# Forget sums broadcast by DMA and masked on GpSimd, in place of two TensorE products for each pair of heads

## The chip, the cores and the metric

The kernel runs on one core of a Trainium2 chip. A core has five engines with instruction streams of their own: TensorE (PE in the profile; PEld is its weight load), VectorE (DVE), ScalarE (ACT), GpSimd (POOL) and SyncE (SP), which here only issues DMAs. Each engine takes its instructions in order, and semaphores order the engines among themselves. The metric is device time in microseconds (us) of one execution; lower is better.

## The reference, cut to what matters

Two layers over 256 tokens of width 1024. Each layer has eight heads of sparse attention (called NSA), eight heads of forgetting attention (called fox) and an MLP with squared ReLU. The change touches the fox heads:

```
log_f = log_sigmoid(f_logits + f_bias)
cum = cumsum(log_f, axis=1)                      # one row of 256 sums for each head
logits = q @ k.T * scale + cum[:, q, None] - cum[:, None, k]
p = softmax(where(k <= q, logits, -1e30))
```

The term cum[q] is the same for a whole row, so it drops out of the softmax. What is left to add is, for each head, one row of -cum[k] that is the same for all 128 queries of a tile, and the causal mask. The kernel works with scores times 8 and undoes it by a factor of -0.125.

## The kernel before, in words

The tokens form two tiles of 128 rows. All weights are split into two parts (whi, wlo) that TensorE multiplies in three products in a reduced float32 form; scores and transposes are full float32 products, which take several passes. A weight unit arrives as a DMA on SP's queue into one of nine buffers with the tag "raw" (RBUFS, line 48). ScalarE copies it into whi, VectorE subtracts to get wlo (`Weights.get`, lines 485 to 508), and the raw buffer is free again.

In each layer: six chunks of the input projection (c0 to c5), the sparse and the forgetting attention interleaved with the later chunks, the output projection (eight units w_out 0 to 7; the first four are worked in between the attention steps, the last four behind them), and the MLP. The attention runs over a list `flat` (line 1322) of 16 NSA tiles and 8 fox tiles. Step i issues the scores of tile i, scales tile i-1, transposes tile i-2, and multiplies with the values from tile i-3; `fill` puts pieces of the stream of chunks and w_out units between them. For a tile, VectorE does the mask-add (`tensor_tensor_reduce` in `scores`, lines 1197 to 1200: score plus mask, times -0.125, with the row minimum), ScalarE the exps, VectorE the scaling, TensorE the three transposes. `side` (line 1324) puts further work behind certain steps; the forget sums stand behind step 8.

The forget sums before (`forget_sums`, line 1023): two products give the running sums in PSUM, with each head's row repeated every 32 rows; ScalarE copies them into hi (reduced form) and rest, and VectorE makes of these the tile cum, in which alternating blocks of 32 rows hold the high and the low part. In `fox_scores` (line 1157) a pair of heads gets its scores by eight float32 passes on 64-row tiles, and then, for each head, one 64x384 product of selr (a column that picks the head's rows, high and low) with cum adds the row of sums to all 128 rows in PSUM.

The order of the instructions is not that of the code. A Recorder keeps every operation; all are issued at line 404, so that line stands in every row of the profile, and groups are told apart by tiles. `schedule` (line 297) is a list scheduler over modelled durations (`_cost`, line 446; for a DMA the bytes over 360 per ns, line 453, plus LATE). It takes buffers of one tag in the order in which the code first used them (`fits`, line 326), so a later raw buffer is never handed out ahead of an earlier one. `order` (line 282) keeps the best of five passes. The result is fixed when the kernel is built.

Of the kernel before, what the change touches and what calls it, by code (L numbers as in the profile page):

```python
# [18 lines left out]
F32 = mybir.dt.float32  # L19
F32R = mybir.dt.float32r  # L20
AF = mybir.ActivationFunctionType
# [114 lines left out]
class View:  # L136
# [21 lines left out]
    def bitcast(self, dtype):  # L158
        return self._with(lambda ap: ap.bitcast(dtype), dtype=dtype)

    def mask(self):
        m = np.zeros(self.buf.size, bool)
        m[self.ix.ravel()] = True
        return m
# [13 lines left out]
class Recorder:  # L178
    def __init__(self, nc, tc):
        self.nc, self.tc = nc, tc  # L180
        self.ops, self.fifo, self.key, self.hot, self.lane, self.group = [], {}, None, False, None, None
        self.after = None
        for e in ("tensor", "vector", "scalar", "sync"):
            setattr(self, e, _Engine(self, e))

    def tile(self, pool, shape, dtype, name, tag=None, bufs=1, psum=False):
# [110 lines left out]
    def schedule(self):  # L297
# [5 lines left out]
        for op in self.ops:  # L303
            op.missing, op.ready, op.start = len(op.deps), 0.0, None
            for b in op.bufs:
                left[b] = b.ops
        waiting = {e: [] for e in ("tensor", "vector", "scalar", "sync")}
        busy = dict.fromkeys(waiting, 0.0)
        bus, tiled = 0.0, (P, P)
        for op in self.ops:  # L310
# [135 lines left out]
def _cost(op, views):  # L446

    out = op.args[0] if op.args else op.kw["out"]
    n = int(np.prod(out.shape[1:]))
    part = 100 * (out.shape[0] < P)  # L450
    if op.engine == "sync":
        v = views[0][1]
        return v.shape[0] * int(np.prod(v.shape[1:])) * 4 / 360.0
    if op.engine == "tensor":
        if op.name == "stretch":
            side = P // min(op.tile)
            return sum(_product(*x[:2], side) for x in op.args[2][::side])
        return _product(op.name, op.args, 1)
    if op.engine == "vector":
        if op.name == "reciprocal":  # L460
            return 60 + 6.5 * n
        if op.name == "tensor_reduce":
            n = int(np.prod(op.args[1].shape[1:]))
        fast = op.name in ("tensor_copy", "tensor_scalar", "memset") and not any(v.buf.psum for _, v in views)
        aps = sum(isinstance(v, View) for v in op.args[2:4]) if op.name == "tensor_scalar" else int(
            op.name == "scalar_tensor_tensor" and isinstance(op.args[2], View))
        return 68 + part + 64 * aps + n * (0.52 if fast else 1.04) + 10 * (op.name == "tensor_tensor_reduce")
    src = op.args[1]
    aps = sum(isinstance(op.kw.get(k), View) for k in ("bias", "scale", "accum_out"))
    return n / 1.2 + (55 if src.buf.psum else 92) + 93 * aps  # L470
# [52 lines left out]
def trunk(nc, A, consts_in, out, sbp, pp):  # L523
    def tile(shape, dtype, name, tag=None, bufs=1):
        return nc.tile(sbp[(tag or name) not in OPERANDS], shape, dtype, name, tag, bufs)
# [251 lines left out]
        if k == 0:  # L777
            nc.vector.tensor_copy(gcol, gcol0)

    selr = tile([P, 8], F32R, name="selr")  # L780
    ident_r = tile([P, P], F32R, name="identr")
    r_mix = [None, None]
    carry = None
# [1 line left out]
    for l in range(DEPTH):  # L785
# [143 lines left out]
        def hidden_gelu(s):  # L929
            u, z = T["gu" + s], T["gz" + s]  # L930
            nc.vector.tensor_scalar(z, z, 1.0, None, op0=OP.add)
            nc.vector.reciprocal(z, z)
            h = small([P, 2, 32], "gh")
            nc.vector.tensor_mul(h, u, z)
            T["gh" + s] = h
# [86 lines left out]

        def forget_sums():


            ps = psum("s")
            f = [x.rearrange("p a b -> p (a b)") for x in lf]
            nc.tensor.matmul(ps[:, :S], f[0], cst[:, C_TRI:C_TRI + S], start=True, stop=False)
            nc.tensor.matmul(ps[:, P:S], f[1], cst[:, C_TRI:C_TRI + P], start=False, stop=True)
            cum = tile([P, 384], F32R, name="cum", tag="cum")  # L1030
            two = tile([P, 2, S], F32R, name="two", tag="rl", bufs=2)
            hi, rest = two[:, 0], two[:, 1].bitcast(F32)
            nc.scalar.activation(hi, ps[:, :S], AF.Copy)
            nc.scalar.activation(rest, ps[:, :S], AF.Copy, scale=cst[:, C_REST:C_REST + 1])
            for o, n in ((0, P), (P, S)):
                nc.vector.scalar_tensor_tensor(cum[:, o:o + n], hi[:, :n].bitcast(F32), cst[:, C_REST + 1:C_REST + 2],
                                               rest[:, :n], op0=OP.mult, op1=OP.add)
            T["cum"] = cum


        def in_chunk(c, evac, by_token=False):
# [114 lines left out]

        def fox_scores(pair):


            ps = [psum("s") for _ in range(2)]  # L1160
            rows = [slice(par * HD, par * HD + HD) for par in range(2)]
            with nc.stretch():
                for o, n, q0 in ((0, 128, 0), (128, 256, 128)):
                    for par, h in enumerate(rows):
                        nc.tensor.matmul(ps[par][:, o:o + n], T["fqT"][h, pair, q0:q0 + P], T["fkT"][h, pair, 0:n],
                                         start=o == 0, stop=False, skip_group_check=True)
                for par, h in enumerate(rows):
                    i = 2 * pair + par
                    nc.tensor.matmul(ps[par][:, 0:384], selr[h, i:i + 1].to_broadcast([HD, P]), T["cum"][h],
                                     start=False, stop=True, skip_group_check=True)  # L1170
            return [(x[:, 0:128], x[:, 128:384]) for x in ps]

        def nsa_scores(e):
# [11 lines left out]
        def scores(e):  # L1185
            kind, pair, par, br = e[:4]
            if kind == "fox":
                if par == 0:
                    T["sc"] = fox_scores(pair)
                ps = T["sc"][par]  # L1190
            else:
                if br == 1:
                    T["sc"] = nsa_scores(e)
                ps = T["sc"][br - 1]
            p = small([P, 384], "pr", 3)
            st = small([P, 4], "st", 4)
            for a, b, t in SEGS:
                nc.vector.tensor_tensor_reduce(
                    out=p[:, a:b], in0=ps[t], in1=cst[:, C_MASK + 256 - (b - a):C_MASK + 256], op0=OP.add, op1=OP.min,
                    scale=-0.125, scalar=3.0e38, accum_out=st[:, t:t + 1])  # L1200
            for a, b, t in SEGS:
                nc.scalar.activation(p[:, a:b], p[:, a:b], AF.Exp, scale=-1.0, bias=st[:, t:t + 1],
                                     accum_out=st[:, 2 + t:3 + t])
            return p, st
# [74 lines left out]
                        r_mix[t] = rsqrt_sum(*squares_of_x(t, "rm"))  # L1279
        row_scales()  # L1280
        if first:
            nc.scalar.activation(selr, cst[:, C_SEL:C_SEL + 8], AF.Copy)
            nc.scalar.activation(ident_r, ident, AF.Copy)

        fill(4)
# [30 lines left out]
        for t in range(NT):  # L1316
# [5 lines left out]
        flat = [("nsa", pair, par, br) for pair in range(4) for par in range(2) for br in (1, 2)]  # L1322
        flat += [("fox", pair, par, 0) for pair in range(4) for par in range(2)]
        side = {0: lambda: fill_to("c3"), 1: compressed_exp, 2: lambda: (compressed_scale(), hidden_T("v")),
                3: lambda: (compressed_T(), hidden_gelu("v")),
                6: compressed_v, 7: compressed_vT, 8: forget_sums, 14: lambda: fill_to("c4"), 17: lambda: fill_to("c5")}
        st = {}
        pTs = {}
        o = None
# [1 line left out]
        for i in range(len(flat) + 4):  # L1331
            if 0 <= i - 1 < len(flat):
                scale(flat[i - 1], *st[i - 1])
            if i < len(flat):
                st[i] = scores(flat[i])
                if i == 15:
                    done.add("nsa")
                    g_post, g_pre2 = load_gains(("g_post_mix", l), ("g_pre_mlp", l))
            fill(1)
            if i in side:  # L1340
                side[i]()
                fill(1)
            if 0 <= i - 2 < len(flat):
                pTs[flat[i - 2]] = probs_T(st.pop(i - 2)[0], i % 2, flat[i - 2])
            fill(1)
            j = i - 3
            if 0 <= j < len(flat) and flat[j][2] == 1 and flat[j][3] != 1:
                kind, pair, par, br = flat[j]
                if pair % 2:
                    o = psum("o")  # L1350
                    if br:
                        nc.tensor.matmul(o, T["vbig"][:, pair // 2], T["pcT"][pair // 2], start=True, stop=False,
                                         skip_group_check=True)
                    cols = lambda q: [(q // 2) * HD] * 2 if br else [2 * q * HD, 2 * q * HD + HD]
                    pv(o, [[([pTs.pop((kind, q, x, b)) for x in range(2)], (fV, vS, vW)[b], cols(q))
                            for b in ((1, 2) if br else (0,))] for q in (pair - 1, pair)], not br)
                    o_evac(o, kind, pair)
            if i >= 12 or i % 2:
                fill(1)
# [203 lines left out]
```

## Time and profile before

| | us |
|---|---|
| median of 3 runs | 622.77 (622.66 to 622.86) |
| the profiled execution, device time | 622.19 |
| its span, first to last instruction | 620.4 |
| VectorE busy | 472.5 |
| ScalarE busy | 382.3 |

The granted clock of TensorE was 0.999 on average. The span leaves out 1.8 us around the first and last instruction. In the profile, out<-in names what an instruction writes and reads; x16 is a count; a timeline row has start, duration, engine, operation, tiles and shape. DMA rows of the page give the median time from issue to landing. A matmul row's duration is from its issue to its modelled end; such products overlap, so their price is the distance between starts.

### The profile page before, as it was taken

The numbers are of one execution on the slowest core, as the hardware profiler recorded it, in microseconds if no ns is written. First come the engines' busy times: TensorE is split into PE (matmuls) and PEld (weight loads), VectorE is DVE, ScalarE is ACT, GpSimd is POOL, SyncE is SP. The second block draws the span as 40 slices with busy tenths as digits, with TensorE's granted clock in tenths as the row PEclk, the third lists the DMA queues.
The fourth block names the chain that finished last, engine by engine and source line by source line (L and its number), as shares of the span: only waits on it lengthen the run. The fifth ranks groups of instructions, "written<-read, shape, count | busy, mean of one in ns | idle before, by whom it ended". The sixth has DMA issues, their size and how long they took to land.

```text
span 620.4 us, 9937 instructions
## 1 busy us (share of the span) xinstructions
PE 612.6 (99%) x3572; PEld 518.6 (84%) x3572; DVE 472.5 (76%) x1043; ACT 382.3 (62%) x730; POOL 0.2 (0%) x4
## 2 busy tenths in 40 slices
PE   9999999999999999999999999999999999999995
PEld 6989987788888888888888998777888888888884
DVE  6889999889976567557598999987996575566544
ACT  7766777577655456555466758765776455556522
POOL 0000000000000000000000000000000000000000
PEclk9999999999999999999999999999999999999999
DMA  8988535218765666664347783532386665655001
GB/s 322 403 312 312 219 105 202 102 37 303 255 189 186 187 204 198 182 197 140 106 139 251 267 328 101 171 104 69 115 296 209 197 196 176 203 190 187 31 1 68
DMA packets 33601, 115.69 MB, mean 186 GB/s; under 512 B 3984, under 2 KB 4112, under 8 KB 33552
## 3 DMA queue, kind: packets, MB, share of 16 engines
q1 hardware_dynamic: 33552, 115.06, 55.5%
q8 instruction: 28, 0.46, 0.3%
q14 instruction: 21, 0.17, 0.1%
HBM read 114.00 MB, written 1.05 MB: 185 GB/s over the span
## 4 chain that ended last, share of the span: by engine, by line
PE 98%; DMA 1%; DVE 0%; ACT 0%; issue 0%; DVEq 0%; SPq 0%
PE s L404 35%; PE acc L404 31%; PE x L404 25%; PE o L404 7%; DMA first<-in_first_dram 1%; DVE x L404 0%; DVE m L404 0%; DVEq L1559 0%; ACT whi L404 0%; DVE rsqrt L404 0%; ACT xT L404 0%; SPq L404 0%; ACT rl L404 0%; DVEq L404 0%
## 5 line engine op out<-in xcount | busy, mean ns | idle before, releaser
L404 DVE TENSOR_TENSOR wlo<-wraw,whi 128x1024 fp32r<-128x1024 f32 (+1 forms) x188 | 225.5, 1201 | 98.7 <-ACT whi L404 58.6
L404 ACT ACTIVATE whi<-wraw 128x1024 fp32r<-128x1024 f32 (+1 forms) x188 | 194.8, 1041 | 106.4 <-PE acc L404 73.5
L404 PE MATMUL s<-xT,whi 128*128 128x512 f32 x448 | 106.5, 390 | 0.0
L404 PEld LDWEIGHTS s<-xT,whi 128*128 128x128 f32 x448 | 83.4, 188 | 16.8
L404 PE MATMUL x<-whi,aT 128*128 128x512 f32 x256 | 88.6, 390 | 0.0
L404 PE MATMUL acc<-whi,aT 128*128 128x512 f32 x256 | 88.3, 389 | 0.0
L404 PEld LDWEIGHTS s<-xT,wlo 128*128 128x128 f32 x448 | 57.4, 191 | 2.2
L404 PE MATMUL s<-xT,wlo 128*128 128x256 f32 x448 | 58.1, 283 | 0.0
L404 PEld LDWEIGHTS acc<-whi,aT 128*128 128x128 f32 x256 | 48.0, 188 | 10.0
L404 PEld LDWEIGHTS x<-whi,aT 128*128 128x128 f32 x256 | 48.1, 188 | 9.6
L404 ACT ACTIVATE pr<-pr,st 128x256 f32<-128x256 f32 (+1 forms) x96 | 42.9, 448 | 19.6 <-DVE st L404 19.3
L404 PE MATMUL x<-wlo,aT 128*128 128x512 f32 x128 | 50.0, 390 | 0.0
L404 PE MATMUL acc<-wlo,aT 128*128 128x512 f32 x128 | 49.9, 390 | 0.0
L404 PE MATMUL acc<-xT,whi 128*128 128x256 f32 x256 | 49.6, 288 | 0.0
L404 PEld LDWEIGHTS acc<-xT,whi 128*128 128x128 f32 x256 | 40.1, 190 | 1.5 <-issue 0.4
L404 PE MATMUL acc<-whi,xT 128*128 128x512 f32 (+1 forms) x128 | 37.5, 353 | 0.0
L404 PE MATMUL acc<-xT,wlo 128*128 128x256 f32 x128 | 36.4, 284 | 0.0
L404 PE MATMUL x<-whi,xT 128*128 128x512 f32 x112 | 36.2, 396 | 0.1
L404 ACT ACTIVATE h<-s 128x256 f32<-128x256 f32 x56 | 21.2, 378 | 16.0 <-PE s L404 16.0
L404 ACT ACTIVATE rl<-h 128x512 f32<-128x512 f32 x28 | 17.7, 633 | 18.0 <-DVE h L404 18.0
L404 PEld LDWEIGHTS acc<-wlo,aT 128*128 128x128 f32 x128 | 24.0, 188 | 5.0
L404 ACT ACTIVATE rl<-x 128x512 f32<-128x512 f32 x24 | 14.7, 612 | 21.8 <-PE x L404 16.7
(221 smaller groups left out, 961.3 us busy)
## 6 DMA issues: line engine op xcount, KB each, us to landing
wraw<-in_w_up_dram SPq DMA_DIRECT2D x64, 512.0 KB, 3.7
wraw<-in_w_down_dram SPq DMA_DIRECT2D x64, 512.0 KB, 3.7
wraw<-in_w_in_dram SPq DMA_DIRECT2D x36, 512.0 KB, 5.1
wraw<-in_w_out_dram SPq DMA_DIRECT2D x16, 512.0 KB, 6.8
w<-in_cmp_w_k_dram SPq DMA_DIRECT2D x8, 512.0 KB, 5.2
w<-in_cmp_w_v_dram SPq DMA_DIRECT2D x8, 512.0 KB, 5.4
first<-in_first_dram SPq DMA_DIRECT2D x7, 384.0 KB, 6.0
wraw<-in_w_in_dram SPq DMA_DIRECT2D x8, 288.0 KB, 4.1
```

Of the source, the lines that this page charges most:

```text
L404: getattr(getattr(self.nc, op.engine), name)(*[real(v) for v in args], **{k: real(v) for k, v in kw.items()})
```

## The change

The two products for each pair are gone, with selr and the split of cum into high and low parts. cum is now a plain float32 tile, copied out of PSUM by two ScalarE copies (128 and 256 columns). The forget sums move from behind step 8 to behind step 4. A new function, called ahead of the scores of every even fox step, takes a raw buffer for a bias tile of 128 x 2 x 384, fills each half by a DMA on SP's queue that reads one row of cum for all 128 rows, and lets GpSimd write -1e30 where the causal mask forbids, in two selects. The mask-add of a fox tile reads this bias where it read the mask. The scheduler learns of GpSimd as a fifth engine.

```
+    def to_rows(self, n):
+        return self._with(lambda ap: ap.unsqueeze(1).to_broadcast([1, n, self.ix.size]))
...
-        waiting = {e: [] for e in ("tensor", "vector", "scalar", "sync")}
+        waiting = {e: [] for e in ("tensor", "vector", "scalar", "gpsimd", "sync")}
...
+    if op.engine == "gpsimd":
+        return 200 + 0.72 * n + 10 * int(np.prod(out.shape[1:-1]))
...
-            cum = tile([P, 384], F32R, name="cum", tag="cum")
-            two = tile([P, 2, S], F32R, name="two", tag="rl", bufs=2)
-            hi, rest = two[:, 0], two[:, 1].bitcast(F32)
-            nc.scalar.activation(hi, ps[:, :S], AF.Copy)
-            nc.scalar.activation(rest, ps[:, :S], AF.Copy, scale=cst[:, C_REST:C_REST + 1])
+            cum = tile([P, 384], F32, name="cum", tag="cum")
             for o, n in ((0, P), (P, S)):
-                nc.vector.scalar_tensor_tensor(cum[:, o:o + n], hi[:, :n].bitcast(F32), cst[:, C_REST + 1:C_REST + 2],
-                                               rest[:, :n], op0=OP.mult, op1=OP.add)
+                nc.scalar.activation(cum[:, o:o + n], ps[:, :n], AF.Copy)
             T["cum"] = cum
+
+        def forget_bias(pair):
+
+            b = tile([P, 2, 384], F32, name="bias", tag="raw", bufs=RBUFS)
+            for par in range(2):
+                i = 2 * pair + par
+                nc.sync.dma_start(b[:, par], T["cum"][i:i + 1, :].to_rows(P))
+            for o in (0, 2 * P):
+                nc.gpsimd.affine_select(out=b[:, :, o:o + P], in_=b[:, :, o:o + P], pattern=[[0, 2], [-1, P]],
+                                        compare_op=OP.is_ge, fill=NEG, base=0, channel_multiplier=1)
+            T["fb", pair] = b
...
-                                         start=o == 0, stop=False, skip_group_check=True)
-                for par, h in enumerate(rows):
-                    i = 2 * pair + par
-                    nc.tensor.matmul(ps[par][:, 0:384], selr[h, i:i + 1].to_broadcast([HD, P]), T["cum"][h],
-                                     start=False, stop=True, skip_group_check=True)
+                                         start=o == 0, stop=o > 0, skip_group_check=True)
...
-                    out=p[:, a:b], in0=ps[t], in1=cst[:, C_MASK + 256 - (b - a):C_MASK + 256], op0=OP.add, op1=OP.min,
+                    out=p[:, a:b], in0=ps[t], in1=T["fb", pair][:, par, a:b] if kind == "fox" else
+                    cst[:, C_MASK + 256 - (b - a):C_MASK + 256], op0=OP.add, op1=OP.min,
...
-                3: lambda: (compressed_T(), hidden_gelu("v")),
+                3: lambda: (compressed_T(), hidden_gelu("v")), 4: forget_sums,
-                6: compressed_v, 7: compressed_vT, 8: forget_sums, 14: lambda: fill_to("c4"), 17: lambda: fill_to("c5")}
+                6: compressed_v, 7: compressed_vT, 14: lambda: fill_to("c4"), 17: lambda: fill_to("c5")}
...
+                if 16 <= i < 24 and i % 2 == 0:
+                    forget_bias(i // 2 - 8)
                 st[i] = scores(flat[i])
```

More of the change, by code (lines that the diff above doesn't have):

```diff
@@ L182, in __init__ @@
         self.after = None
-        for e in ("tensor", "vector", "scalar", "sync"):
+        for e in ("tensor", "vector", "scalar", "gpsimd", "sync"):
             setattr(self, e, _Engine(self, e))
@@ L778, in first_xT @@
             nc.vector.tensor_copy(gcol, gcol0)
-    selr = tile([P, 8], F32R, name="selr")
     ident_r = tile([P, P], F32R, name="identr")
@@ L1281, in trunk @@
         if first:
-            nc.scalar.activation(selr, cst[:, C_SEL:C_SEL + 8], AF.Copy)
             nc.scalar.activation(ident_r, ident, AF.Copy)
```

## The prediction, made before the changed kernel ran

> **What bounds the kernel now.** I read the page from the top: busy shares, slices, chain, and then the view of waits for TensorE alone.
>
> ```profile
> PE 612.6 (99%) x3572; PEld 518.6 (84%) x3572; DVE 472.5 (76%) x1043; ACT 382.3 (62%) x730; POOL 0.2 (0%) x4
> PE   9999999999999999999999999999999999999995
> PEclk9999999999999999999999999999999999999999
> DMA  8988535218765666664347783532386665655001
> PE 98%; DMA 1%; DVE 0%; ACT 0%; issue 0%; DVEq 0%; SPq 0%
> ```
>
> ```profile
> PE o L404 <- DVE warm L404: 1.2, 1, 1.2
> ```
>
> The reader is to see that TensorE is the bound from end to end: 612.6 us of a 620.4 us span, 98% of the chain, full clock, and one wait of 1.2 us in the whole run, for the warm-up tile. So a product taken from TensorE is a gain at its full price, and anything new that TensorE has to wait for is a loss at its full price. DMA is half idle on average, which will turn out to be no cover.
>
> **What goes.** Each of the eight pairs of forgetting heads (four in each layer) loses two 64x384 products.
>
> ```profile
> L404 PE MATMUL s<-cum,selr x16: 518/520/523, 96.3 to 416.7; 64*128 64x384 f32 x16
> ```
>
> ```profile
> 95.73 0.93 PE L404 MATMUL s<-fkT,fqT 64*128 64x128 f32 x8
> 96.30 0.53 PE L404 MATMUL s<-cum,selr 64*128 64x384 f32 x2
> 96.76 0.50 PE L404 MATMUL x<-whi,oT 128*128 128x512 f32 x1
> ...
> 97.34 0.40 PE L404 MATMUL x<-whi,oT 128*128 128x512 f32 x1
> 97.58 0.40 PE L404 MATMUL acc<-whi,oT 128*128 128x512 f32 x1
> 97.81 0.40 PE L404 MATMUL x<-whi,oT 128*128 128x512 f32 x1
> ```
>
> The 520 ns is a latency of pipelined products, not their price. From the start of the pair to the next product are 0.46 us (96.30 to 96.76), but that holds the tail of the score products ahead and the change back to 128x128 tiles, which stay. What leaves is the streaming of 384 columns, for both halves side by side. Products of 512 columns stand 0.235 us apart (97.34, 97.58, 97.81), so 384 columns are 0.18 us. I take 0.18 (upper end 0.46): 8 x 0.18 = **1.4 us off TensorE** (upper end 3.7). Off the bound go four VectorE instructions (415 ns each) and two of four ScalarE copies become narrower; neither engine is waited for, so I cost them at nothing.
>
> ```profile
> L404 DVE SCALAR_TENSOR_TENSOR cum<-two,cst x4: 346/415/485, 82.3 to 387.5; 128x256 fp32r<-128x256 f32 x2, 128x128 fp32r<-128x128 f32 x2
> ```
>
> **What comes.** Per layer: eight DMAs on SP's queue, each writing one 1.5 KB row of cum to all 128 rows (192 KB), and eight selects on GpSimd. The mask-add reads bias in place of the mask: same instruction, same size, nothing. The four bias tiles take four of the nine "raw" buffers that hold arriving weights.
>
> Where they stand decides. In the order of the changed program, SP's queue in each layer has w_out 0, then the first bias DMA, and the remaining seven w_out loads between and behind the others; ahead of w_out 4 stand all eight bias DMAs and w_out 1 to 3. Buffers are handed out in that order, so no later load can overtake. Before, nothing held those loads:
>
> ```profile
> 55.18 6.26 SPq L404 DMA_DIRECT2D wraw<-in_w_out_dram  x8
> ```
>
> All eight w_out loads of layer 0 were issued from 55.2 to 61.4 us. Now the first bias DMA waits for cum, and w_out 1 to 7 are queued behind it on SP. The forget sums move up: in layer 0 they stand right ahead of the third tile's transposes, in layer 1 some five products ahead of them.
>
> ```profile
> 69.25 0.49 PE L404 MATMUL s<-cst,pr 128*128 128x128 f32 x3
> ```
>
> ```profile
> 373.05 0.49 PE L404 MATMUL s<-cst,pr 128*128 128x128 f32 x3
> ```
>
> ```profile
> 78.31 0.38 PE L404 MATMUL s<-cst,lf 128*128 128x256 f32 x1
> ```
>
> ```profile
> 79.53 0.38 ACT L404 ACTIVATE two<-s 128x256 fp32r<-128x256 f32 x1
> ```
>
> Before, the copy out of PSUM ended 1.6 us after the sums began (78.31 to 79.91). So cum is ready at 69.25 + 1.6 = 70.9 us, and in layer 1, five products of some 0.18 us earlier, at 373.05 - 0.9 + 1.6 = 373.7 us.
>
> **The disputed price: one bias DMA.** No row of before shows a transfer whose source is one SBUF row. Below: the gains are one HBM row written to all rows, 512 KB, and land in 3.8 us, as fast as a plain weight load (3.7 us on the page).
>
> ```profile
> gains<-in_g_pre_mlp_dram SPq DMA_DIRECT2D x1, 512.0 KB, 3.8
> ```
>
> ```profile
> wraw<-in_w_up_dram SPq DMA_DIRECT2D x64, 512.0 KB, 3.7
> ```
>
> ```profile
> 20.00:40.00 20.00, 20.00 (x139) 16.75 (x139) 16.81 (x50) 13.59 (x27) 0.00 (x0) 1.00 0.91 343
> ```
>
> At the 343 GB/s of this busy stretch, 512 KB take 1.5 us of the 3.7, the other 2.2 being latency; a bias DMA would take 0.57. Above: all 16 engines draw on one row, and if that row feeds them no faster than one engine moves data, the price is sixteenfold.
>
> ```profile
> GB/s 322 403 312 312 219 105 202 102 37 303 255 189 186 187 204 198 182 197 140 106 139 251 267 328 101 171 104 69 115 296 209 197 196 176 203 190 187 31 1 68
> ```
>
> The second slice, with engines at 9 tenths or more, moves 403 GB/s, or 25.2 per engine: 196,608 B / 25.2 = **7.8 us** (8.3 with the 343 at 0.91). I take the upper end, 7.8. [...]
>
> **The sum.** w_out 4 lands after cum + 8 x 7.8 + 4 x 1.5 (w_out 1 to 4) + 2.2: at 70.9 + 62.4 + 6.0 + 2.2 = 141.5 us in layer 0, and 373.7 + 70.6 = 444.3 us in layer 1. Who waits: ScalarE, in order. In its changed order the split of w_out 4 stands in layer 0 between an exp of the twelfth NSA tile and the first oT copy, and in layer 1 right ahead of that copy.
>
> ```profile
> 83.98 0.28 DVE L404 CUSTOM_DVE_ANT_0 pr<-s,cst 128x128 f32<-128x128 f32 x1
> ```
>
> ```profile
> 87.28 0.60 ACT L404 ACTIVATE oT<-o 128x512 fp32r<-128x512 f32 x1 [1.93 <-PE o L404]
> ```
>
> ```profile
> 392.44 0.60 ACT L404 ACTIVATE oT<-o 128x512 fp32r<-128x512 f32 x1 [1.15 <-PE o L404]
> ```
>
> So it is wanted at about 85 (between 84.0 and 87.3) and 391.4 us (392.44 less one split of 1.04 us). Queued behind it on ScalarE are the exps whose tiles TensorE transposes next. They have some slack:
>
> ```profile
> 85.06 0.66 DVE L404 TENSOR_SCALAR pr<-pr,st,gate 128x256 f32<-128x256 f32 x2
> ```
>
> ```profile
> 90.16 0.49 PE L404 MATMUL s<-cst,pr 128*128 128x128 f32 x3
> ```
>
> ```profile
> 392.08 0.66 DVE L404 TENSOR_SCALAR pr<-pr,st,gate 128x256 f32<-128x256 f32 x2
> ```
>
> ```profile
> 395.33 0.38 PE L404 MATMUL s<-cst,pr 128*128 128x128 f32 x2
> ```
>
> 4.4 us (85.72 to 90.16) and 2.6 us (392.74 to 395.33). TensorE's stall: 141.5 - 85 - 4.4 = 52 in layer 0; 444.3 - 391.4 - 2.6 = 50 in layer 1. By then all four bias tiles have landed, so the forgetting scores add nothing, and later weights meet an empty queue. The profiled execution took 622.19: 622.19 - 1.4 + 102.4 = 723.2, and since the median lies 0.6 above it, **724 us**. Each us on the price of a bias DMA is worth 16 us; with the slack the stall vanishes below 1.3 us in layer 0 ((85 + 4.4 - 70.9 - 8.2) / 8) and 1.5 in layer 1.
>
> **Rivals.**
> *The broadcast is cheap* (the side of faster). At 0.57 us each, w_out 4 lands at 70.9 + 4.6 + 8.2 = 83.7 and 386.5, both ahead of 85 and 391.4. No stall: 622.19 - 1.4 = 620.8, or 621.4 on the median, 0.22% down; it decides below 1.3 us a DMA. For it: the gains row. Against: that source is not SBUF.
> *Slow, but weights pass.* If packets of w_out slip past waiting broadcasts, only the fourth pair's mask-add waits.
>
> ```profile
> 112.78 0.40 DVE L404 CUSTOM_DVE_ANT_0 pr<-s,cst 128x256 f32<-128x256 f32 x1
> ```
>
> ```profile
> 418.23 0.42 DVE L404 CUSTOM_DVE_ANT_0 pr<-s,cst 128x256 f32<-128x256 f32 x1
> ```
>
> Bias 3 lands at 70.9 + 62.4 + 2.2 and is masked 0.8 later (two selects, each put at VectorE's 0.4 for 256 columns): 136.3, 23.5 late; 439.1 in layer 1, 20.9 late. 622.2 - 1.4 + 44.4 = 665, 666 on the median. A price halfway (4 us) with no passing gives about as much: 21.7 + 19.9 late, 663. One case.
> *Cheap, but GpSimd is in VectorE's way.* The before trace has no such select; bounds are nothing and 16 x 0.42 = 6.7 us of VectorE held up, less the 1.7 it is spared: up to 626. [...]
> That the products don't go is no rival: the changed order has none of the sixteen.
>
> **Chances.** Forecast 0.60 (own range 710 to 750: 8.3 us a DMA gives 732, w_out loads that hide wholly under the broadcasts give 12 less, 712; the rest upward is for TensorE's clock after a stall, which no row shows); between 0.17; cheap 0.19, of which 0.16 is faster and 0.03 the same, since 1.4 is hardly over the 0.2% (1.2 us) that a measurement can tell; GpSimd 0.04, half the same. Faster 0.16, same 0.05, slower 0.79. The range runs from the cheap case to 745: what it leaves out are the forecast's upper end and the cheapest of the cheap, under 0.2.
>
> **What would show it.** Right: bias DMAs that land over 7 us apart; ScalarE waiting on DMA wraw from in_w_out; TensorE idle in two stretches of some 50 us at 75 to 140 and 380 to 490; few GB/s there. Wrong: bias landing as fast as weights, and TensorE still 99% busy (cheap); ScalarE's splits on time but VectorE's mask-adds waiting (weights pass).

## The result, and the profile after

The changed kernel takes 712.03 us in the median of 5 runs (711.82 to 712.25), the kernel before 622.66 (622.28 to 622.86) beside it. The ratio is 1.1437, with a 95% interval of 1.142 to 1.1453. The profiled execution took 712.03 us and its span is 709.7, so 89.3 us more lie between the first and last instruction than in the kernel before (620.4).

The page after, in the order in which that of before was read: busy shares, slices, chain.

```profile
PE 627.9 (88%) x3556; PEld 527.0 (74%) x3556; DVE 473.0 (67%) x1039; ACT 380.4 (54%) x729; POOL 6.8 (1%) x20
PE   9999743499999999999999994518999999999996
...
PEclk9999867699999999999999998757999999999999
...
GB/s 333 390 300 66 56 76 41 243 220 94 200 292 194 195 187 182 205 188 145 119 169 245 210 11 82 45 110 255 182 60 271 211 202 189 195 181 196 99 1 60
...
PE 83%; DMA 12%; DVE 2%; SPq 1%; ACT 1%; issue 1%; DVEq 0%; ACTq 0%
```

TensorE has two holes, one in each layer, at slices 5 to 8 and 25 to 28 of 40 (a slice is 17.7 us, so 71 to 142 and 426 to 497 us). From slice 4 to 7 the DMAs move 41 to 76 GB/s, from slice 25 to 27 45 to 110. The granted clock falls with the holes, to 6 and 5 tenths in the lowest slices. The chain, 98% TensorE before, is now 12% DMA. The waits of TensorE:

```profile
PE s L407 <- DVE st L407: 30.4, 4, 12.7
PE s L407 <- DVE pr L407: 26.8, 3, 14.7
PE s L407 <- ACT prT L407: 9.1, 1, 9.1
PE o L407 <- ACT prX L407: 7.6, 1, 7.6
```

These are 73.9 us of waits that didn't exist before. They name VectorE and ScalarE, but those are only the last links. What ScalarE itself waited for is in its timeline (start, duration, then in brackets its idle time and what ended it), for layer 0 and the end of the hole in layer 1:

```profile
70.26 0.38 ACT L407 ACTIVATE cum<-s 128x256 f32<-128x256 f32 x1
81.58 1.06 ACT L407 ACTIVATE whi<-wraw 128x1024 fp32r<-128x1024 f32 x1 [5.64 <-DMA wraw<-in_w_out_dram]
96.11 1.06 ACT L407 ACTIVATE whi<-wraw 128x1024 fp32r<-128x1024 f32 x1 [11.85 <-DMA wraw<-in_w_out_dram]
111.37 1.06 ACT L407 ACTIVATE whi<-wraw 128x1024 fp32r<-128x1024 f32 x1 [12.95 <-DMA wraw<-in_w_out_dram]
129.80 1.06 ACT L407 ACTIVATE whi<-wraw 128x1024 fp32r<-128x1024 f32 x1 [15.47 <-DMA wraw<-in_w_out_dram]
131.75 0.57 ACT L407 ACTIVATE oT<-o 128x512 fp32r<-128x512 f32 x1
...
418.56 0.55 ACT L407 ACTIVATE cum<-s 128x256 f32<-128x256 f32 x2
...
478.38 1.06 ACT L407 ACTIVATE whi<-wraw 128x1024 fp32r<-128x1024 f32 x1 [9.80 <-DMA wraw<-in_w_out_dram]
479.34 0.58 ACT L407 ACTIVATE oT<-o 128x512 fp32r<-128x512 f32 x1
```

The cum copies end at 70.64 us. The splits of w_out 1 to 4 start the moment their loads land, and the first oT copy, at 87.28 us before, comes at 131.75: 44.5 us late. In layer 1 it comes at 479.34 for 392.44, 86.9 late, and the later oT copies there are 89 late. With 89.3 us at the end, each layer loses some 44.5 us. It is not one wait in a layer: four splits in a row come late, and TensorE stops nine times in the two layers, at most for 14.7 us.

GpSimd's selects show when pairs of broadcasts land, since each starts with the second landing of its pair:

```profile
87.71 0.77 POOL L407 TENSOR_SCALAR_AFFINE_SELECT bias<-bias 128x256 f32<-128x256 f32 x2 [87.27 <-DMA bias<-cum]
101.61 0.76 POOL L407 TENSOR_SCALAR_AFFINE_SELECT bias<-bias 128x256 f32<-128x256 f32 x2 [13.14 <-DMA bias<-cum]
116.03 1.22 POOL L407 TENSOR_SCALAR_AFFINE_SELECT bias<-bias 128x256 f32<-128x256 f32 x2 [13.65 <-DMA bias<-cum]
128.76 0.77 POOL L407 TENSOR_SCALAR_AFFINE_SELECT bias<-bias 128x256 f32<-128x256 f32 x2 [11.52 <-DMA bias<-cum]
```

From the first pair to the fourth are six broadcasts in 41.05 us: 6.84 us each. This distance is the ruler for all experiments below. Counted from the end of the cum copies (70.64) to the landing of the eighth broadcast (issued at 105.5 us, landed 23.0 later), with w_out 1 to 3 between, it is 57.9 us for eight, 7.2 each, or 27 GB/s, the figures in the expectations. The DMA view of 82 to 101 us, 40 slices of 0.48 us each, shows the engines busy and moving next to nothing:

```profile
GB/s 26 29 26 32 23 29 23 32 23 32 23 29 32 23 32 23 29 23 29 23 32 19 39 87 260 320 312 160 111 26 36 19 36 16 39 19 32 29 39 112
...
q1 hardware_dynamic: 552, 1.08, 87.3%
```

16 engines at 87% move 16 to 39 GB/s together, but for the few slices in which the weight w_out 2 passes at up to 320, and the last.

### The profile page after: what moved, and what is told of

It is laid out like the page before. It is cut to its first block, busy times and chain, and to the rows that moved or that the text cites. A ratio compares the mean times of both kernels' runs of the same rounds, so it can differ in the third digit from the quotient of the medians.

```text
span 709.7 us, 9972 instructions
## 1 busy us (share of the span) xinstructions
PE 627.9 (88%) x3556; PEld 527.0 (74%) x3556; DVE 473.0 (67%) x1039; ACT 380.4 (54%) x729; POOL 6.8 (1%) x20
## 2 busy tenths in 40 slices
DMA packets 35905, 118.84 MB, mean 167 GB/s; under 512 B 4240, under 2 KB 6416, under 8 KB 35856
## 4 chain that ended last, share of the span: by engine, by line
PE 83%; DMA 12%; DVE 2%; SPq 1%; ACT 1%; issue 1%; DVEq 0%; ACTq 0%
PE s L407 30%; PE acc L407 25%; PE x L407 22%; DMA wraw<-in_w_out_dram 12%; PE o L407 6%; SPq L407 1%; DVE wlo L407 1%; DVE pr L407 0%; ACT whi L407 0%; ACT pr L407 0%; DVE x L407 0%; DVE m L407 0%; DVEq L1565 0%; DVE oT L407 0%; DVE rsqrt L407 0%
## 5 line engine op out<-in xcount | busy, mean ns | idle before, releaser
L407 PE MATMUL s<-cst,pr 128*128 128x128 f32 x144 | 27.1, 307 | 65.2 <-DVE st L407 29.2
L407 PEld LDWEIGHTS s<-cst,pr 128*128 128x128 f32 x144 | 19.6, 157 | 73.4 <-issue 55.4
L407 DVE RECIPROCAL st<-st 128x2 f32<-128x2 f32 x48 | 7.5, 159 | 69.6 <-ACT pr L407 69.5
L407 ACT ACTIVATE pr<-pr,st 128x256 f32<-128x256 f32 (+1 forms) x96 | 42.6, 446 | 17.6 <-DVE st L407 17.6
L407 PE MATMUL acc<-whi,xT 128*128 128x512 f32 (+1 forms) x128 | 41.9, 388 | 0.0
## 6 DMA issues: line engine op xcount, KB each, us to landing
bias<-cum SPq DMA_DIRECT2D x16, 192.0 KB, 17.6
```

What stands on the lines that cost most here:

```text
L407: getattr(getattr(self.nc, op.engine), name)(*[real(v) for v in args], **{k: real(v) for k, v in kw.items()})
```

## The experiments

All eleven are variants of the changed kernel, except the fifth, which starts from the kernel before. Ratios are to the kernel before, timed on the same chip.

### A source of many rows

```
-                nc.sync.dma_start(b[:, par], T["cum"][i:i + 1, :].to_rows(P))
+                nc.sync.dma_start(b[:, par], T["cum"])
```

> The sixteen bias DMAs read all 128 rows of cum, one row for each row written, in place of one row 128 times; number, size, queue, order, selects and buffers stay. The sums added to the scores are then the wrong ones, so this leaves the right forget term out. Theory A (one SBUF row supplies its 128 readers at some 27 GB/s, 7.2 us a DMA, and all that is queued behind waits): bias DMAs land like weights of their size, under 3 us from the one before, no split on ScalarE waits for w_out, and the time is 620.5 to 622.5. Theory B (the price lies in the wait of SP's queue for cum, in the raw buffers held, or in GpSimd): 690 or more.

Measured: 621.67 us, ratio 0.9983 (0.9973 to 0.9992). Two rows of the page:

```profile
PE 611.6 (99%) x3556; PEld 517.2 (83%) x3556; DVE 472.9 (76%) x1039; ACT 380.6 (61%) x729; POOL 7.9 (1%) x20
...
bias<-cum SPq DMA_DIRECT2D x16, 192.0 KB, 5.4
```

The time is the one of Theory A. Same bytes, same queue, same order, same selects and mask-adds, and both holes are gone. The whole loss sits in what the DMA reads. GpSimd's selects are all there and TensorE is 99% busy, so the rival that put GpSimd in VectorE's way has nothing left to explain.

### Two rows by turns

```
-                i = 2 * pair + par
+                i = 2 * pair + par + 64 * par
```

The sums of a head stand in rows i, i+32, i+64 and i+96 of cum, so this reads the same numbers from another row.

> Nothing is left out: the second head of each pair reads row i+64 of cum, which holds the same sums as row i, so that consecutive broadcasts draw on rows far apart. Theory A1 (the limit is of the place where the row lies, and neighbours in the queue overlap as the w_out loads do, which cost no extra time beside the broadcasts): two broadcasts run side by side, w_out 4 lands some 29 us earlier in each layer, 645 to 675. Theory A2 (each broadcast runs through alone at 7.2 us, whatever row it reads): 708 to 716, as the changed kernel.

Measured: 685.48 us, ratio 1.1008 (1.0988 to 1.1029), between the two expectations. The selects, first and last pair:

```profile
86.51 0.77 POOL L407 TENSOR_SCALAR_AFFINE_SELECT bias<-bias 128x256 f32<-128x256 f32 x2 [86.07 <-DVE pr L407]
...
116.02 0.77 POOL L407 TENSOR_SCALAR_AFFINE_SELECT bias<-bias 128x256 f32<-128x256 f32 x2 [5.50 <-DMA bias<-cum]
```

Six broadcasts in 29.5 us: 4.92 us each, for 6.84, not half of it. Two rows 64 apart gave more than one row (40 GB/s for 28.7), but not twice as much. What held them there was not found.

### Sixteen rows

The tile of forget gates holds each head sixteen times instead of four, so the same two products leave a head's sums in rows i, i+8, ..., i+120, and a broadcast reads each of these eight times.

```
+    def spread(self, i):
+        return self._with(lambda ap: ap[i:P:8, :].unsqueeze(1).to_broadcast([16, 8, self.ix.size]))
...
-                nc.sync.dma_start(b[:, par], T["cum"][i:i + 1, :].to_rows(P))
+                nc.sync.dma_start(b[:, par], T["cum"].spread(i))
```

> Nothing is left out: the sums are kept in all 16 groups of 8 rows in place of 4 groups of 32, and each broadcast reads 16 rows, each 8 times. Theory A: 16 times less asked of one row, under 2 us a DMA, 620.5 to 622.5, about 1 us faster than the kernel before. Theory C (reading a row several times is slow as such, or a DMA with a step of zero in its source is): 690 or more.

Measured: 622.21 us, ratio 1.0 (0.9992 to 1.0009). The DMA view from 72 to 86 us, slices of 0.35 us:

```profile
GB/s 0 22 206 176 206 116 187 257 339 398 372 373 259 299 278 246 257 328 329 334 291 284 296 225 317 217 353 312 262 288 240 271 237 274 294 238 320 228 325 293
...
q1 hardware_dynamic: 1724, 3.68, 98.3%
```

The same broadcasts, with the weights between them, run at 200 to 400 GB/s, and the holes are gone. So reading a row several times is not slow as such (Theory C). The 1 us under the kernel before that Theory A also named did not come.

### Over device memory

```
-            T["cum"] = cum
+            T["cum"] = nc.tile(sbp["hbm"], [8, 384], F32, "cumh", "cumh", DEPTH)
+            nc.sync.dma_start(T["cum"], cum[0:8, :])
```

> Nothing is left out: the eight rows of cum are written to HBM once a layer (12 KB), and the sixteen broadcasts read them there, as the gains are. Theory A: a broadcast lands like the gains did for its size, one more store and its landing (about 2 us) before the first; 620.5 to 623. Theory C: as slow as from SBUF, 690 or more.

Measured: 623.0 us, ratio 1.0007 (0.9999 to 1.0016); span 620.7. The page's row of the broadcasts:

```profile
bias<-cumh SPq DMA_DIRECT2D x16, 192.0 KB, 5.8
```

Here the source is one row again, 128 times, but not in SBUF, and the holes are gone. So "one row read 128 times" isn't dear by itself (5.8 us to land, for 17.6 in the changed kernel); one row of SBUF is.

### Only the products removed

From the kernel before:

```
-                                         start=o == 0, stop=False, skip_group_check=True)
-                for par, h in enumerate(rows):
-                    i = 2 * pair + par
-                    nc.tensor.matmul(ps[par][:, 0:384], selr[h, i:i + 1].to_broadcast([HD, P]), T["cum"][h],
-                                     start=False, stop=True, skip_group_check=True)
+                                         start=o == 0, stop=o > 0, skip_group_check=True)
```

> The kernel before with only the sixteen 64x384 products taken out of the fox scores; the sums are still made but not added, so the forget term is left out of the result. If a pair of products is worth 0.18 us of TensorE, as the prediction has it, the time is 8 x 0.18 = 1.4 us under the kernel before: 621.2 us beside 622.6. If the pair is worth its whole distance of 0.46 us, it is 3.7 us under: 618.9. If other work fills the place, because the products wait for nothing and the scores' evacuation sets the pace, nothing is gained: 622.6. The versions with a cheap broadcast had 0.9 us (one that reads many rows) and nothing (one that reads sixteen) under the kernel before, so 0.9 to 1.4 is expected, and the rest of those versions' loss would be the broadcasts' own.

Measured: 620.81 us beside 622.76, ratio 0.9972 (0.9961 to 0.9982), so 1.1 to 2.4 us less; span 619.1 for 620.4.

```profile
PE 611.3 (99%) x3556; PEld 517.7 (84%) x3556; DVE 472.5 (76%) x1043; ACT 381.8 (62%) x730; POOL 0.2 (0%) x4
```

TensorE is busy 1.3 us less (612.6 before), as the 8 x 0.18 us had it. This is all that taking the products away can gain.

### The forget sums later

```
-                3: lambda: (compressed_T(), hidden_gelu("v")), 4: forget_sums,
-                6: compressed_v, 7: compressed_vT, 14: ...
+                3: lambda: (compressed_T(), hidden_gelu("v")),
+                6: compressed_v, 7: compressed_vT, 8: forget_sums, 14: ...
```

> The changed kernel with the forget sums behind step 8 again, where the kernel before has them; all else as changed. If the stall is the end of a chain that starts when cum is ready and runs at the pace of the broadcasts, then w_out 4 lands later by what cum is later: about 9.3 us in layer 0 (80.0 for 70.6) and 11 us in layer 1, and the whole takes some 20 us more than the changed kernel: 732 us (725 to 736). If the stall came of the number of transfers on the queue or of the shared buffers, whenever cum is ready, the time stays near 712 us.

Measured: 710.9 us, ratio 1.1415 (1.1395 to 1.1436). The 732 us did not come, though the landing did move. ScalarE's timeline:

```profile
92.70 0.58 ACT L407 ACTIVATE oT<-o 128x512 fp32r<-128x512 f32 x1
...
138.88 1.06 ACT L407 ACTIVATE whi<-wraw 128x1024 fp32r<-128x1024 f32 x1 [13.34 <-DMA wraw<-in_w_out_dram]
...
146.01 0.57 ACT L407 ACTIVATE oT<-o 128x512 fp32r<-128x512 f32 x1
```

and the second oT copy of the kernel before:

```profile
104.77 0.60 ACT L404 ACTIVATE oT<-o 128x512 fp32r<-128x512 f32 x1 [1.26 <-PE o L404]
```

w_out 4 is split at 138.88 in place of 129.80, 9.1 us later, as expected. But its split now stands ahead of the second oT copy and not of the first, which comes at 92.7 us, ahead of w_out 2 to 4. The second copy is at 146.01 for 104.77 before, 41.2 late (the fourth 43.0, for 44.8 in the changed kernel). The scheduler had moved the want with the sums: the split starts 7.1 us ahead of the second copy, which is 97.6 us in the kernel before, and in the changed kernel 1.95 us ahead of the first, which is 85.3. So it is wanted some 12 us later, and lands 9.1 us later. The expectation held the want fixed, and that was its mistake: the stall is landing less want, and an edit of the order moves both.

### A queue of their own

```
-                    getattr(getattr(self.nc, op.engine), name)(
+                    own = name == "dma_start" and any(x.name == "cum" for x in op.bufs)
+                    getattr(getattr(self.nc, "gpsimd" if own else op.engine), name)(
```

> The changed kernel with the sixteen broadcasts issued by GpSimd on its own queue; order, tiles and buffers are the same, nothing is left out. No w_out load stands behind a broadcast any more. If the weights were late because their queue was held, they now land as in the kernel before (w_out 4 near 80 us instead of 130), and only the mask-add of the fourth pair waits for its row: eight broadcasts at 7.2 us from 70.6 us, 0.8 us of selects, so 129.4 us for 112.8 in layer 0 and 14 us late in layer 1: 621.5 + 31 = 652 us (640 to 665), the prediction's case of weights that pass. If the weights are late because the broadcasts' packets hold the DMA engines themselves, the weights land late as well and the time stays at 700 to 715 us. If GpSimd's own issuing is slow, the broadcasts land more than 7.2 us apart and the fourth pair is later than 129 us.

Measured: 690.64 us, ratio 1.1101 (1.1081 to 1.1121), between the two. ScalarE's timeline, and the DMA view from 76 to 128 us (queue: packets, MB, share of the 16 engines' time; q0 has the broadcasts, q1 is SP's):

```profile
87.47 0.60 ACT L408 ACTIVATE oT<-o 128x512 fp32r<-128x512 f32 x1 [0.32 <-PE o L408]
129.41 1.06 ACT L408 ACTIVATE whi<-wraw 128x1024 fp32r<-128x1024 f32 x1 [34.44 <-DMA wraw<-in_w_out_dram]
138.88 0.60 ACT L408 ACTIVATE oT<-o 128x512 fp32r<-128x512 f32 x1 [1.16 <-PE o L408]
```

```profile
q0 software_dynamic: 479, 1.43, 86.4%
q1 hardware_dynamic: 428, 1.35, 6.6%
```

Both theories were half right. w_out 0 to 5 were issued ahead of the broadcasts and are on time, so the first oT copy is (87.47). But w_out 6, issued at 78.57 us on a queue with no broadcast in it, lands at 129.4, 50.8 us later and behind the last broadcast. Its queue got 6.6% of the engines' time and the broadcasts' 86.4% (0.7 and 92.0% from 76 to 90 us). Counted in packets the two are nearly even, 428 to 479: a packet of a broadcast kept its engine some twelve times as long as one of SP's queue. The split of w_out 6 stands ahead of the second oT copy, which is 34.1 us late (104.77 before); twice that is 68.2, and 622.8 + 68.2 = 691. So it isn't the order on SP's queue alone that holds the weights. The broadcasts hold the DMA engines, and weights that are issued after them wait on a queue of their own too.

### Shorter broadcasts

```
-                nc.sync.dma_start(b[:, par], T["cum"][i:i + 1, :].to_rows(P))
-            for o in (0, 2 * P):
+                nc.sync.dma_start(b[:, par, P:], T["cum"][i:i + 1, P:].to_rows(P))
+            for o in (2 * P,):
...
-                    ... if kind == "fox" else
+                    ... if kind == "fox" and t else
```

> The changed kernel with broadcasts of 256 columns of cum in place of 384 (128 KB for 192 KB, the same 128 packets each); the first query tile, whose 128 columns are not fetched, reads the mask alone, so the forget term is left out there, and one of the two selects of a pair. The order on the queue is the same. If a broadcast's price is its bytes through one row's way out (27 GB/s), it falls from 7.2 to 4.8 us; the eight take 38.6 us in place of 57.9, w_out 4 lands 19.3 us earlier in each layer, and the whole takes 712.0 - 38.6 = 673 us (668 to 680). If the price is per packet (about 56 ns for each of 128 packets, whatever their length), nothing changes: 712 us.

Measured: 674.29 us, ratio 1.0827 (1.0808 to 1.0847), as the first theory had it: 37.7 us less than the changed kernel for the expected 38.6.

```profile
82.93 0.44 POOL L407 TENSOR_SCALAR_AFFINE_SELECT bias<-bias 128x256 f32<-128x256 f32 x1 [82.48 <-DVE st L407]
...
109.76 0.41 POOL L407 TENSOR_SCALAR_AFFINE_SELECT bias<-bias 128x256 f32<-128x256 f32 x1 [7.67 <-DMA bias<-cum]
```

Six broadcasts in 26.8 us: 4.47 us each for 128 KB, 29.3 GB/s; the 192 KB at 6.84 us are 28.7 GB/s. The price goes with the bytes, not with the packets, whose number is the same (35905 on both pages).

### Four rows

```
+    def spread(self, i):
+        return self._with(lambda ap: ap[i:P:32, :].unsqueeze(1).to_broadcast([4, 32, self.ix.size]))
```

The broadcast reads the four rows of a head that cum holds anyway.

> The changed kernel, but each broadcast reads the four rows of cum that hold the same head's sums (i, i+32, i+64, i+96), each 32 times, in place of one row 128 times. Nothing else differs, and nothing is left out. If four rows have four ways out of 27 GB/s each, a broadcast takes 1.8 us, the eight 14.4, and w_out 4 lands near 70.6 + 14.4 + 4 = 89 us, just when the slack ends (85 + 4.4): 622 to 626 us. If rows 32 apart share a way as rows 64 apart partly did (two of them brought the distance from 7.2 to 5.5, not to 3.6), the distance is 3 to 4 us, w_out 4 lands near 100, and some 10 us in each layer are lost: 635 to 655 us. If the number of rows doesn't matter, 712 us.

Measured: 667.16 us, ratio 1.0719 (1.0703 to 1.0735): none of the three, the second being nearest. The selects (81.79 to 106.37 us) give 4.10 us for a broadcast, just above its 3 to 4 (the 7.2 and 5.5 that it starts from are 6.84 and 4.92 by the selects). The expectation's own sum then gives 70.6 + 32.8 + 4 = 107.4 us for w_out 4, which is split at 107.76. What no case had foreseen is how little of the engines' time is used. First the page's count of packets of the changed kernel, then this version's DMA view from 79 to 91 us (slices of 0.3 us), then its own count:

```profile
DMA packets 35905, 118.84 MB, mean 167 GB/s; under 512 B 4240, under 2 KB 6416, under 8 KB 35856
```

```profile
DMA  9279998222222222312297669994222122222212
GB/s 247 70 207 369 355 234 210 60 51 41 46 56 46 51 46 46 79 31 41 51 193 164 191 246 387 416 352 121 82 77 67 41 46 61 67 72 61 56 41 51
```

```profile
DMA packets 35713, 118.84 MB, mean 179 GB/s; under 512 B 4048, under 2 KB 6224, under 8 KB 35664
```

Where only a broadcast runs, the engines are not at 87% as in the changed kernel but at 2 tenths: as an estimate, about four of sixteen work, each at some 12 of the 48 GB/s. There are 192 packets under 512 bytes fewer, 12 for each of the 16 broadcasts, as many as the engines that would stay idle. That a broadcast with a source written as four rows by 32 reads was put on four engines is thus the author's estimate; no view shows single engines. But an engine moved 25.2 GB/s in the kernel before, so the number of engines alone doesn't explain 48 GB/s for the four. Whether the four rows or the four engines set it is not shown: four rows on sixteen engines were not tried.

### Sixteen rows, sums later

> The version with broadcasts from sixteen rows, with the forget sums behind step 8 again, where the kernel before has them; nothing is left out. With only the products gone 620.8 us were measured, which is the floor; the sixteen-row version with early sums took 622.2 and lost its 1.4 us ahead of the forgetting tiles (its first oT copy stood 2.1 us later than with the products merely gone). If the early sums cost that, this version takes 620.8 to 621.3, 0.2 to 0.3% under the kernel before. If the sixteen-fold sums or the broadcasts cost it, 622 to 622.5, the same as before. If cum is now too late for the queue (ready 8 us later, eight broadcasts of 0.6 us, then the weights), 623 to 630.

The edits are those of the sixteen rows and of the later sums together. Measured: 630.53 us, ratio 1.012 (1.0103 to 1.0137), just past the third case.

```profile
398.32 1.06 ACT L410 ACTIVATE whi<-wraw 128x1024 fp32r<-128x1024 f32 x1 [2.00 <-DMA wraw<-in_w_out_dram]
401.94 1.06 ACT L410 ACTIVATE whi<-wraw 128x1024 fp32r<-128x1024 f32 x1 [2.17 <-DMA wraw<-in_w_out_dram]
```

ScalarE waits for w_out again, two us at a time in layer 1 and once 3.3 us in layer 0: even quick broadcasts now start 8 us later (12 in layer 1), with the weights still behind them. So the early sums were not what kept the sixteen-row version from its 1.4 us; without them it loses more. Of the 7.0 us between the spans of the two profiled executions (628.5 and 621.5), 4.4 are waits of TensorE (4.9 for 0.5, beside the warm-up's) and 2.7 longer busy time (615.6 for 612.9). How much of these comes from the late weights, and how much from the changed order, was not followed.

### Four rows, sums later

> The version with broadcasts from four rows and the forget sums behind step 8. The one-row version with late sums had w_out 4 landing 9.1 us later and yet took 1.2 us less, because its order on ScalarE wants w_out 4 some 10 us later. If the stall is landing less want, this version takes no more than the four-row version with early sums, whatever that takes: 621 to 624 us if four rows suffice there; if that one stalls, this one is within 3 us of it.

The edits are those of the four rows and of the later sums together. Measured: 668.52 us, ratio 1.0736 (1.0714 to 1.0757), 1.4 us above the version with early sums: within the expected 3, though not "no more". w_out 4 is split 8.8 us later (116.53 for 107.76), but ahead of the second oT copy and not of the first, so landing and want have moved together again.

## Why the prediction was right, step by step

The mechanism was the one forecast, in every link that the last part of the prediction named: the selects show the broadcasts 6.8 us apart (a little under the 7 that was asked for), ScalarE waits for wraw from in_w_out, TensorE has its two holes, and few GB/s move in them. The holes lie at 71 to 142 and 426 to 497 us. The size was 12 us too large. Several terms were off and partly cancel: a broadcast and the loads were put too high, the delay behind the landing too low. That the prediction's case of hidden loads names the measured 712 us is therefore luck.

- **The gain, 1.4 us: right.** With the products alone removed, TensorE's busy time falls by 1.3 us and the median by 1.1 to 2.4.
- **GpSimd, VectorE and ScalarE at nothing: right.** The many-row version has all the new instructions and takes 621.67 us. A select takes 0.41 us in the median (at most 0.86), as put. The mask-add that reads bias is no longer than the one that read the mask (281 to 425 ns; 0.40 to 0.42 us for 256 columns before):

```profile
L407 DVE CUSTOM_DVE_ANT_0 pr<-s,bias x32: 281/346/425, 142.5 to 508.6; 128x256 f32<-128x256 f32 x16, 128x128 f32<-128x128 f32 x16
```

- **cum ready at 70.9 us: right** (70.64). In layer 1 the last copy ends at 419.1, which is 373.7 plus layer 0's delay of 44.5, and 0.9.
- **A broadcast at 7.8 us: 6.84 us.** The choice of the upper end, one SBUF row as good as one engine's rate, was right, though no row of before decides it; the rate was 28.7 GB/s and not 25.2. Eight broadcasts were 7.7 us cheaper. Two rows by turns brought 6.84 down to 4.92.
- **Four w_out loads at 1.5 us each and 2.2 us to land, 8.2 us in all: 4.4.** Eight broadcasts at 6.84 us from 70.64 end at 125.4, and w_out 4 is split at 129.80. The 6.84 already hold what w_out 2 and 3 cost between the broadcasts: with no weights in between (the own queue, selects at 89.33 to 128.56 us) a broadcast took 6.54 us. So the loads were 3.8 us too dear.
- **w_out 4 at 141.5 us: 129.8**, by these two terms (7.7 and 3.8) and cum, which was 0.3 early.
- **Wanted at 85 with 4.4 us of slack behind it: 5 us too kind in layer 0.** 129.8 - 85 - 4.4 = 40.4, but the first oT copy is 44.5 us late, and the first product of w_out on TensorE 45.5. What stood between the landing and that product, then the same product in the kernel before:

```profile
131.95 1.21 DVE L407 TENSOR_TENSOR wlo<-wraw,whi 128x1024 fp32r<-128x1024 f32 x1
133.07 1.25 DVE L407 TENSOR_SCALAR pr<-pr,st,gate 128x256 f32<-128x256 f32 x4
133.88 0.88 PE L407 MATMUL s<-cst,pr 128*128 128x128 f32 x3 [14.71 <-DVE pr L407]
138.38 0.40 PE L407 MATMUL x<-whi,oT 128*128 128x512 f32 x1
```

```profile
92.91 0.39 PE L404 MATMUL x<-whi,oT 128*128 128x512 f32 x1
```

  The transposes, at 90.16 before, come at 133.88, 43.7 us late and 3.3 more than the sum had. The slack was counted from the end of the scaling. After the landing the split itself (1.0 us), the exps, and on VectorE the low part of a weight (131.95, 1.2 us) come first, which now stands ahead of the scaling. From the transposes to the first product of w_out are then 4.50 us, for 2.75 before (90.16 to 92.91): 1.8 more for nearly the same products, without a wait between. The windows view (start and end, length, then busy us and count of PE, PEld, DVE, ACT, POOL, then clock) shows a lower granted clock there, 0.60 from 130 to 140 us:

```profile
90.00:110.00 20.00, 6.30 (x33) 3.84 (x32) 2.42 (x8) 2.31 (x7) 0.76 (x2) 0.67 0.87 83
130.00:140.00 10.00, 6.12 (x24) 5.20 (x25) 7.22 (x28) 7.89 (x23) 0.00 (x0) 0.60 0.70 260
140.00:150.00 10.00, 10.00 (x79) 7.14 (x78) 9.58 (x35) 6.96 (x23) 0.00 (x0) 1.00 0.81 243
```

  In the whole run TensorE is busy 627.9 us, 16.6 more than with the products merely gone (611.3), and 73.9 us of new waits plus 15.3 of longer busy time (627.9 - 612.6) are the 89.2 that were lost. The prediction had named the clock as a possible addition and put no price on it.
- **"Weights pass": wrong, and more so than thought.** Even on a queue of their own, weights issued behind the broadcasts passed so slowly that they landed behind the last (w_out 6 after 50.8 us).
- **"Cheap": the wrong side of its own point.** The point from which it decides, 1.3 us a broadcast, fits the runs: with sixteen rows the selects of the first three pairs are some 3.7 us apart. Less a w_out load of 1.5 us, an estimate from 512 KB at 343 GB/s, that is 1.1 us a broadcast, and no stall is left.

What stays open: no version with a broadcast reached the 620.8 us of the kernel without the products. Many rows gave 621.7, sixteen 622.2, the detour over device memory 623.0, though TensorE waits in each for some 2 us or less. Part of it lies outside the instructions: the time exceeds the span by 1.8 us in the kernel without the products and by 2.3 to 2.5 in these three. With many rows the span is 619.3 us in the median, for 619.05 without the products; where the 0.6 us outside come from was not followed. The many-row and the sixteen-row version both run in the order of the changed kernel, the detour in another, so what lies between those two is not order. What of the rest is order and what the granted clock was not separated. Also open is whether the limit belongs to the single row or to a place in SBUF that several rows share. No run beats the kernel before with the whole computation in it.

## What to carry to other kernels

Price a DMA by what it reads, not by its bytes alone: here a broadcast that reads one row of SBUF moved 29 GB/s on sixteen engines that were 87% busy, while the same bytes from sixteen rows went along with the weights at 200 to 400. What took the stall away was to let the product that makes the row write it to sixteen rows (622.21 us for 712.03). Then ask what is issued behind it, on a second queue too, and when that is wanted: the stall is landing less want, and both move when the order does. And weigh the gain first: here sixteen products were worth 1.4 us, so no detour by DMA could have won more than 0.2 to 0.3%.

## What the runs showed of the hardware

- One row of SBUF fed sixteen DMA engines with 28.7 GB/s (384 columns) and 29.3 GB/s (256 columns); two rows 64 apart, by turns, with 40.
- A second queue gave no quick way past: from 76 to 128 us the broadcasts on GpSimd's queue held 86.4% of the engines' time with 479 packets, SP's queue got 6.6% with 428, and a load issued on it at 78.57 us took 50.8 us to land.
- The share of the engines' time went with the way in which the source was written: one row by 128 reads ran at 87.3%; four rows by 32 at 2 tenths and 48 GB/s, with 12 packets under 512 bytes fewer for each broadcast; sixteen rows by 8, with weights between them, at 98.3%.
- The clock that TensorE was granted was 0.67 from 90 to 110 us, where it was busy for 6.3 of 20 us, 0.60 from 130 to 140, where it took up work again, and 1.00 in the 10 us after that.
